# Three short segments of A moved from GpSimd's queue to Sync's, in fp32, in a tiled matmul with leaky ReLU

## The chip, the cores and the metric

One core of one Trainium2 chip. The metric is the device time of one execution in microseconds (us), slowest core, here the only one.

## The reference

```python
m, k, n = 4096, 4096, 4096
a = randn(m, k).astype(float32); b = randn(k, n).astype(float32); alpha = 0.01

def reference(a, b, alpha):
    x = np.matmul(a, b)
    return np.where(x > 0, x, alpha * x)
```

The kernel multiplies in bf16 and accumulates in fp32; 8192 matmuls of 128x128 by 128x512 are needed.

## The kernel before

The output is cut into regions of 512 rows by 1024 columns. The contraction of 4096 is cut into *segments*; the first unit of 1024 is split into two short segments of 512, so that the first two regions can begin early:

```python
SEGS = [(0, 0, 4), (0, 4, 4), (1, 0, 8), (2, 0, 8), (3, 0, 8)]   # unit, first chunk, chunks
TURNS = [(0, [0]), (1, [0]), (0, [1]), (1, [1, 2]), (0, [2, 3]), (1, [3, 4]), (0, [4])]
WHERE = {1: [4, 4, 4, 4], 2: [2, 2, 4, 4], 4: [3, 5, 5, 5]}
```

`TURNS` is the order in which the first two regions (half h of the rows, 0 or 1) take their segments s. One pair (h, s) is a *step*; A(h, s) is its part of A. The first step is (0, 0), the second (1, 0), the third (0, 1), the fourth (1, 1), the fifth (1, 2). A short step is 32 matmuls, a long one 64.

The first step is loaded by Sync and ScalarE's queue in fp32 and rounded by DVE and ScalarE. Everything after it comes over GpSimd's queue, which rounds fp32 to bf16 in the transfer (its packet records before the change hold 1.57 MB of 256-byte writes for the 3.15 MB of fp32 of the three short segments). A is turned ahead of the matmuls: four strips of 32 partitions each are loaded, and DVE transposes 32x32 blocks of pairs of bf16 values (0.42 us for 128x256 pairs).

```python
def load_a(mb, h, s, mt, tiles):
    ...
    def fetch():
        a16 = a16_pool.tile([P, 4 * tiles, kw // 4], BF16, name="a16")
        for q in range(4):
            src = a[row:row + tiles * P, k0 + q * kw // 4:k0 + (q + 1) * kw // 4]
            to = a16[32 * q:32 * q + 32]
            nc.gpsimd.dma_start(to, src.rearrange("(g i) w -> i g w", i=32))
        held.append(a16)

    def turn(t0=0, t1=tiles):
        dst = new_a(mb, h, u)[...]
        nc.vector.transpose(dst..., held[0][:, 4 * t0:4 * t1, :]...)
    return fetch, turn

def load_b(pi, n, s, c):
    u, c0, _ = SEGS[s]
    nc.gpsimd.dma_start(new_b(pi, u)[:, c0 + c, :], b_rows(n, s, c))
```

After a step, `spill` copies its eight PSUM banks out (ScalarE and DVE, or an add on DVE), and the next step may use them. GpSimd starts when A's first rows are rounded, and the second step's strips are turned between the spills of the first:

```python
        if (what, i) == ("a", MT - 1):
            nc.gpsimd.tensor_copy(x[:, :1], a_rounded[:, i, :1])
...
turns[1][0](0, 1)
for mt in range(MT):
    spill(0, mt, banks)
    if mt == 0:
        turns[1][0](1, 2)
turns[1][1]()
for fetch in fetches[2]:
    fetch()
```

In the steps that follow, `WHERE` says behind which group of matmuls the next step's tiles are turned.

## Time and profile before

| | before |
|---|---|
| time, median of the first three runs | 1784.02 us (1783.79 to 1784.41) |
| span in the profile | 1782.6 us |
| TensorE busy | 1775.6 us |
| waits of TensorE from 8.68 us on, all ahead of 47 us | 0.68 + 0.99 + 0.81 = 2.48 us |

A row of a timeline is the start in us, the length, the engine and source line, the operation with its tiles, the count, and in brackets the idle time ahead and what ended it. PE is TensorE, ACT is ScalarE, DVE is VectorE, POOL is GpSimd and SP is Sync; a q behind a name is that engine's queue of instructions. A CAST rounds fp32 to bf16. A transfer *lands* when its last byte is there and whoever waits for it may go on; its packets are the single pieces that the profile records. The granted clock is the share of full speed at which TensorE ran. A profile is one execution; its first 7 us vary by about half a microsecond from one to the next, so the start times of two profiles are compared with that in mind. The lines that carry the argument stand in the prediction below.

### The profile page before, as it was taken

How to read it: one execution, taken by the hardware profiler on the slowest of the kernel's cores; microseconds unless marked ns; L12 is line 12 of the kernel's file. 1: busy time of each engine (PE TensorE's matmuls, PEld its weight loads, DVE VectorE, ACT ScalarE, POOL GpSimd, SP SyncE). 2: the span in 40 equal slices, each digit the busy share in tenths (PEclk: the TensorE clock that was granted, in tenths of full speed). 3: DMA queues.
4: the chain of work that ended last, by engine and by line, in shares of the span. 5: the costliest groups of instructions: out<-in, count | busy, mean ns of one | idle time of the engine just before them, and what ended most of it. 6: DMA issues, size and time to landing. Idle time of an engine off the chain costs nothing.

```text
span 1782.6 us, 18214 instructions
## 1 busy us (share of the span) xinstructions
PE 1775.6 (100%) x8251; PEld 807.3 (45%) x8251; DVE 147.1 (8%) x141; ACT 150.3 (8%) x267; POOL 372.5 (21%) x679
## 2 busy tenths in 40 slices
PE   9999999999999999999999999999999999999999
PEld 4444444444444444444444444444444444444444
DVE  4530000022000000002200000000220000000000
ACT  2010000000000000000000000000000000000011
POOL 6631200433002020043201202014320110301000
PEclk9999999999999999999999999999999999999999
DMA  9995653988039165398704917449860481835511
GB/s 195 200 246 138 116 132 87 187 128 127 39 95 189 48 119 118 95 195 130 123 26 95 188 48 135 102 103 202 129 121 13 111 173 48 163 73 119 117 48 47
DMA packets 164173, 212.50 MB, mean 119 GB/s; under 512 B 43776, under 2 KB 93056, under 8 KB 164096
## 3 DMA queue, kind: packets, MB, share of 16 engines
q0 software_dynamic: 143360, 141.08, 49.9%
q10 hardware_dynamic: 19440, 67.12, 9.7%
q1 hardware_dynamic: 1296, 3.15, 0.5%
q8 instruction: 64, 1.05, 0.2%
q14 instruction: 13, 0.11, 0.0%
HBM read 285.21 MB, written 67.11 MB: 198 GB/s over the span
## 4 chain that ended last, share of the span: by engine, by line
PE 97%; DMA 2%; POOL 1%; issue 0%; SPq 0%; DVE 0%; ACT 0%; POOLq 0%
PE ps L162 97%; DMA bt<-in_b_dram 1%; POOL a L124 1%; DMA a<-in_a_dram 0%; DMA a_in<-in_a_dram 0%; POOL bt L146 0%; SPq L260 0%; DVE a_rounded L267 0%; ACT o L402 0%; POOL x L312 0%; POOLq L312 0%
## 5 line engine op out<-in xcount | busy, mean ns | idle before, releaser
L162 PE MATMUL ps<-bt,at 128*128 128x512 bf16 x8224 | 1769.4, 378 | 2.6 <-DMA bt<-in_b_dram 2.5
L162 PEld LDWEIGHTS <-at 128*128 128x128 bf16 x8224 | 804.3, 98 | 966.8 <-issue 2.5
L146 POOL DMA_DIRECT2D bt<-in_b_dram x412 | 219.3, 539 | 1078.9 <-PE ps L162 1031.9
L385 ACT ACTIVATE o<-ps 128x512 f32<-128x512 f32 x239 | 130.5, 595 | 1511.1 <-PE ps L162 1436.3
L129 DVE STREAM_TRANSPOSE at<-a 128x1024 uint32<-128x1024 uint32 (+2 forms) x83 | 114.5, 1422 | 1152.4 <-DMA a<-in_a_dram 935.7
L124 POOL DMA_DIRECT2D a<-in_a_dram x260 | 152.4, 591 | 200.9 <-DVE at L129 127.2
L240 DVE TENSOR_TENSOR part<-ps,part 128x512 f32<-128x512 f32 x40 | 25.3, 682 | 31.8 <-PE ps L162 31.8
L247 ACT ACTIVATE o<-part 128x1024 f32<-128x1024 f32 x8 | 8.5, 1057 | 100.5 <-DVE part L240 87.3
L92 PE MATMUL wp<-w 128*128 128x512 bf16 x11 | 4.9, 632 | 1.2 <-DVE x L84 1.2
L242 DVE COPY part<-ps 128x512 f32<-128x512 f32 x8 | 5.2, 670 | 1.7 <-PE ps L162 1.7
L244 ACT COPY part<-ps 128x512 f32<-128x512 f32 x8 | 4.4, 593 | 5.9 <-PE ps L162 4.9
L92 PEld LDWEIGHTS <-w 128*128 128x128 bf16 x11 | 1.5, 144 | 3.7 <-issue 2.5
L278 ACT CAST bt<-b_in 128x512 bf16<-128x512 f32 x4 | 2.5, 619 | 3.9 <-DMA b_in<-in_b_dram 3.9
L274 ACT COPY at<-turned 128x512 bf16<-128x512 bf16 x4 | 2.3, 586 | 0.9 <-PE turned L273 0.7
L273 PEld LDWEIGHTS <-a_rounded 128*128 128x128 bf16 x16 | 1.5, 125 | 1.4 <-DVE a_rounded L267 0.9
L273 PE MATMUL turned<-ident,a_rounded 128*128 128x128 bf16 x16 | 2.0, 264 | 0.1
L267 DVE CAST a_rounded<-a_in 128x512 bf16<-128x512 f32 x4 | 1.7, 427 | 4.7 <-DMA a_in<-in_a_dram 4.6
L278 DVE CAST bt<-b_in 128x512 bf16<-128x512 f32 x4 | 1.7, 426 | 2.9 <-DMA b_in<-in_b_dram 2.9
L312 POOL CAST x<-a_rounded 128x1 f32<-128x1 bf16 x1 | 0.2, 183 | 6.7 <-DVE a_rounded L267 6.7
L89 ACT ACT_TABLE_LOAD x1 | 1.3, 1283 | 1.2 <-PEq L421 1.2
L402 ACT ACTIVATE o<-ps 128x256 f32<-128x256 f32 x2 | 0.8, 383 | 6.0 <-PE ps L162 6.0
L82 DVE MEMSET w<- 128x256 uint32 x1 | 0.3, 272 | 0.9 <-PEq L421 0.9
(8 smaller groups left out, 1.2 us busy)
## 6 DMA issues: line engine op xcount, KB each, us to landing
bt<-in_b_dram POOLq DMA_DIRECT2D x412, 256.0 KB, 7.7
out_dram<-o ACTq DMA_DIRECT2D x120, 512.0 KB, 3.9
a<-in_a_dram POOLq DMA_DIRECT2D x244, 128.0 KB, 5.3
out_dram<-o ACTq DMA_DIRECT2D x14, 256.0 KB, 2.0
b_in<-in_b_dram SPq DMA_DIRECT2D x3, 512.0 KB, 6.7
a_in<-in_a_dram SPq DMA_DIRECT2D x4, 256.0 KB, 5.0
a<-in_a_dram POOLq DMA_DIRECT2D x16, 64.0 KB, 3.1
b_in<-in_b_dram ACTq DMA_DIRECT2D x1, 512.0 KB, 4.7
```

The source lines that it names most:

```text
L92: nc.tensor.matmul(wp, w[:, :P], w, start=True, stop=True)
L124: nc.gpsimd.dma_start(to, src.rearrange("(g i) w -> i g w", i=32))
L129: nc.vector.transpose(dst.rearrange("p c m e -> p c (m e)").bitcast(U32) .rearrange("p c (g i) -> p g c i", i=32), held[0][:, 4 * t0:4 * t ...
L146: nc.gpsimd.dma_start(new_b(pi, u)[:, c0 + c, :], b_rows(n, s, c))
L162: nc.tensor.matmul(ps, plain(t)[:, c, rows] if (mb, h, u) == (0, 0, 0) and c < kc0 else t[:, c // 2, rows, c % 2], bt[pi, u][:, c, cols or ...
L240: nc.vector.tensor_add(kept, banks[mt, nt], kept)
L242: nc.vector.tensor_copy(kept, banks[mt, nt])
L244: nc.scalar.copy(kept, banks[mt, nt])
L247: nc.scalar.activation(o, part[h][:, mt, :], LRELU, alpha=alpha)
L273: nc.tensor.transpose(turned[:, c, :], cols[:, c, :], ident)
L278: copy(b0[:, i, columns(nt)], b_in[:, i, columns(nt)])
L385: nc.scalar.activation(o[:, cols], banks[mt, nt], LRELU, alpha=alpha)
```

## The change

The intent is to relieve GpSimd's queue, whose issues hold up B in the first 47 us (7.35 us of them stand ahead of B's second segment). A(1, 0), A(0, 1) and A(1, 1) come over Sync in fp32; ScalarE rounds them; GpSimd's loads begin behind the last strip of A(1, 0), so that they do not disturb it. The core of the diff:

```diff
-WHERE = {1: [4, 4, 4, 4], 2: [2, 2, 4, 4], 4: [3, 5, 5, 5]}
+WHERE = {1: [2, 2, 3, 3], 2: [1, 1, 3, 3], 4: [3, 5, 5, 5]}
...
+    def load_short_a(h, s, staged, tiles):
+        ...
+        def fetch():
+            for mt in range(0, MT, tiles):
+                row = (h * MT + mt) * P
+                for q in range(4):
+                    src = a[row:row + tiles * P, k0 + q * kw // 4:k0 + (q + 1) * kw // 4]
+                    to = staged[32 * q:32 * q + 32, 4 * mt:4 * (mt + tiles), :]
+                    nc.sync.dma_start(to, src.rearrange("(g i) w -> i g w", i=32))
+        def turn(t0, t1):
+            if not held:
+                held.append(a16_pool.tile([P, 4 * MT, kw // 4], BF16, name="a16"))
+            strips = slice(4 * t0, 4 * t1)
+            nc.scalar.copy(held[0][:, strips, :], staged[:, strips, :])
+            transpose(new_a(0, h, u), s, t0, held[0][:, strips, :])
+        return fetch, turn, held
...
+    short = {
+        (1, 0): load_short_a(1, 0, a_both[:, 1], 2),
+        (0, 1): load_short_a(0, 1, a_more[:, 0], MT),
+        (1, 1): load_short_a(1, 1, a_more[:, 1], MT),
+    }
-        made = pieces_a(0, h, s, 2 if i in (1, 3) else None) if i else []
+        made = [] if i == 0 else [short[h, s][:2]] if (h, s) in short else pieces_a(0, h, s)
...
-        if (what, i) == ("a", MT - 1):
-            nc.gpsimd.tensor_copy(x[:, :1], a_rounded[:, i, :1])
...
     turns[1][0](0, 1)
     for mt in range(MT):
+        if mt + 1 < MT:
+            turns[1][0](mt + 1, mt + 2)
         spill(0, mt, banks)
-        if mt == 0:
-            turns[1][0](1, 2)
-    turns[1][1]()
+    nc.gpsimd.tensor_copy(x[:, :1], short[1, 0][2][0][:, 4 * MT - 1, :1])
```

(The staging tiles `a_both` and `a_more` take slots of the pool of B; the transpose is moved into a helper of its own. Both are left out here.)

More of the change, by code (lines that the diff above doesn't have):

```diff
@@ L110, in k_of, with transpose @@
         return (u * KC + c0) * P, kc * P
+    def transpose(at_tile, s, mt, a16):
+        _, c0, kc = SEGS[s]
+        rows = slice(mt * P, mt * P + 32 * a16.shape[1])
+        dst = at_tile[:, c0 // 2:(c0 + kc) // 2, rows, :]
+        nc.vector.transpose(
+            dst.rearrange("p c m e -> p c (m e)").bitcast(U32)
+            .rearrange("p c (g i) -> p g c i", i=32),
+            a16.rearrange("p g w -> p (g w)").bitcast(U32)
+            .rearrange("p (g j c) -> p g c j", j=32, c=kc // 2),
+        )
     def load_a(mb, h, s, mt, tiles):
@@ L127, in turn @@
         def turn(t0=0, t1=tiles):
-            dst = new_a(mb, h, u)[:, c0 // 2:(c0 + kc) // 2, (mt + t0) * P:(mt + t1) * P, :]
-            nc.vector.transpose(
-                dst.rearrange("p c m e -> p c (m e)").bitcast(U32)
-                .rearrange("p c (g i) -> p g c i", i=32),
-                held[0][:, 4 * t0:4 * t1, :].rearrange("p g w -> p (g w)").bitcast(U32)
-                .rearrange("p (g j c) -> p g c j", j=32, c=kc // 2),
-            )
-        return fetch, turn
+            transpose(new_a(mb, h, u), s, mt + t0, held[0][:, 4 * t0:4 * t1, :])
+        return fetch, turn
+    def load_short_a(h, s, staged, tiles):
+        u, c0, kc = SEGS[s]
+        k0, kw = k_of(s)
+        held = []
+        def fetch():
[12 more added lines that the diff above has]
+        return fetch, turn, held
     def b_rows(n, s, c):
@@ L221 @@
     finals = [max(i for i, step in enumerate(steps) if step[0] == h) for h in range(HALVES)]
+    a_rounded = at_pool.tile([P, MT, kw0], BF16, name="a_rounded", tag="at")
+    a_both = bt_pool.tile([P, 2, 4 * MT, P], FP32, name="a_in", tag="bt")
+    a_in = a_both[:, 0].rearrange("p (m q) w -> p m (q w)", m=MT)
+    b0 = new_b(0, 0)
+    a_more = bt_pool.tile([P, 2, 4 * MT, P], FP32, name="a_more", tag="bt")
+    short = {
[3 more added lines that the diff above has]
+    }
     fetches = []
@@ L248, in spill @@
             nc.scalar.dma_start(place(0, h, pairs[0], mt), o)
-    a_rounded = at_pool.tile([P, MT, kw0], BF16, name="a_rounded", tag="at")
-    a_in = bt_pool.tile([P, MT, kw0], FP32, name="a_in", tag="bt")
     order = [("b", 0)] + [("a", mt) for mt in range(MT)] + [("b", c) for c in range(1, kc0)]
@@ L263 @@
     a0 = new_a(0, 0, 0)
-    b0 = new_b(0, 0)
     def round_a(i):
```

## The prediction

> **What bounds the kernel now.** I read the page's busy table first, then the chain that ended last in order of time, then TensorE's timeline of the first 60 us, then GpSimd's.
>
> ```profile
> span 1782.6 us, 18214 instructions
> PE 1775.6 (100%) x8251; PEld 807.3 (45%) x8251; DVE 147.1 (8%) x141; ACT 150.3 (8%) x267; POOL 372.5 (21%) x679
> ...
> 36.93 9.96 DMA bt<-in_b_dram
> 46.89 0.04 issue
> 46.94 1732.53 PE ps L162 x8058
> ```
>
> The last lines are from the chain. From 46.94 us on it is TensorE alone: 8058 matmuls in 1732.53 us, 215 ns each, with no wait to the end. The change touches only the first two regions and is over before then, so the whole question is **when the matmul that started at 46.94 us starts afterwards**. Call that time T; the new time is 1784.02 - (46.94 - T). Nothing behind it can get shorter.
>
> TensorE's timeline shows what can be won before it:
>
> ```profile
> 8.68 13.45 PE L162 MATMUL ps<-bt,at 128*128 128x512 bf16 x60
> 22.81 13.97 PE L162 MATMUL ps<-bt,at 128*128 128x512 bf16 x64 [0.68 <-DMA bt<-in_b_dram]
> 37.77 8.36 PE L162 MATMUL ps<-bt,at 128*128 128x512 bf16 x38 [0.99 <-DMA bt<-in_b_dram]
> 46.94 13.33 PE L162 MATMUL ps<-bt,at 128*128 128x512 bf16 x61 [0.81 <-DMA bt<-in_b_dram]
> ```
>
> The brackets hold the idle time before a group: 0.68 + 0.99 + 0.81 = **2.48 us**, all for loads of B that GpSimd issues. So T is at the least 46.94 - 2.48 = 44.46, and the change is worth 2.5 us at most, 0.14% of the time.
>
> GpSimd's timeline says why B is late:
>
> ```profile
> 8.01 0.18 POOL L312 CAST x<-a_rounded 128x1 f32<-128x1 bf16 x1 [6.70 <-DVE a_rounded L267]
> 8.59 7.35 POOL L124 DMA_DIRECT2D a<-in_a_dram  x12 [0.40 <-issue]
> 15.93 2.18 POOL L146 DMA_DIRECT2D bt<-in_b_dram  x4
> ...
> 31.89 2.29 POOL L146 DMA_DIRECT2D bt<-in_b_dram  x4
> 34.69 1.86 POOL L146 DMA_DIRECT2D bt<-in_b_dram  x3 [0.51 <-DMA a<-in_a_dram]
> 36.93 0.54 POOL L146 DMA_DIRECT2D bt<-in_b_dram  x1 [0.38 <-DMA a<-in_a_dram]
> ```
>
> Twelve short loads of A cost 7.35 us of issue (0.61 us for each 64 or 128 KB) ahead of B's second segment, and more stand ahead of B's third, whose last part is issued at 36.93 and frees TensorE at 46.94. The stretches show what the transfers reach, in written bytes: 402 GB/s in 6.5-10.5 (Sync, fp32), 107 in 11-16 (short A, 256-byte writes, GpSimd 100% busy), 152 in 25.5-28.5 (short A), 194 in 46.5-56 (long A, 512-byte writes), 209 in 36.5-45 (B, 2 KB writes). GpSimd's loads read twice the bytes that they write.
>
> [...]
>
> **The change part by part.**
>
> *Removed from GpSimd*: the three short segments, 16 loads of 64 KB and 4 of 128 KB, 20 x 0.59 = 11.8 us of issue. In transfer time it is 1.57 MB written, at about 140 GB/s some 11 us.
>
> *Added on Sync*: 16 loads, 3 x 1.05 MB fp32 in 512-byte pieces, behind the loads of B's first segment, which end at 10.8 us. The packet records give 84 ns for 2 KB and 159 ns for 4 KB, so about 9 ns + 37.5 ns per KB: 28 ns for 512 bytes, 295 GB/s on 16 engines (an estimate). [...] With 0.7 us from the last byte to the consumer (last packet of b_in 10.84, cast 11.58), the first pair of tiles of A(1,0) is there at 10.7 + 2.2 + 0.7 = 13.6, the second at 15.8, A(0,1) at 20.2, and A(1,1) at 25 to 28, because it shares with B. The built program lets a load wait for the one eight issues earlier; the last of A(1,0) then waits for b_in's landing at 11.5, which still keeps the queue filled.
>
> *Added on ScalarE*: 12 casts 128x512 fp32 to bf16, 0.62 us each by the row of b_in's cast, 7.4 us. ScalarE has room (10.6 us busy of the first 44.5), but the casts stand in its order between the copies that free PSUM banks, 0.59 us each, so a late strip holds up a bank. *DVE*: 12 transposes of 0.42 us, instead of 10 in the same work.
>
> *Moved*: GpSimd begins behind the fourth cast of A(1,0). On ScalarE: two casts 13.6 to 14.84, bank copy to 15.43, cast from 15.8 to 16.42, bank copy to 17.0, cast to 17.63. Then GpSimd's small copy, and 0.4 us as before: first load of B at about 18.3, against 15.93. First bytes 1.5 us later (8.59 to 10.1 before): 19.8, against 18.7.
>
> *Sum for T by the transfers*: [...]the other 0.95 MB take 3.3 us at 295. GpSimd's own, up to the last of B's third segment: B second 1.05 MB / 208 = 5.0, long A 1.05 / 192 = 5.5, B third 2.1 / 208 = 10.1, together 20.6. 19.8 + 3.3 + 20.6 + 0.7 = 44.4. The same sum for before, from 18.7: 20.6 + 3.75 for A(1,1) + 0.7 = 43.8, while it really was 46.9[...]. I take half of it, as the queue mixes fewer small loads: **T about 45.9**, 1.0 us gained.
>
> *Sum by ScalarE and DVE*: A(0,1) at 20.2 has to be cast and turned by 22.1, where its step begins. Two casts (21.4), bank copy (22.0), two casts (23.3), bank copies (23.9, 24.5): tile 3 can start at about 24.5 to 25, where an unbroken TensorE wants it at 23.4. That is 1.1 to 1.6 us of new wait; A(1,1) at 28 would add about 1. They do not add to a later wait for B but take its place, as TensorE then asks later: 44.46 + 1.3 = 45.8, or 46.8 with both. Both sums fall near 46, hence T = 45.9 and 1784.02 - 1.04 = **1783.0 us**.
>
> **The rivals.** (a) *All waits hidden.* If strips run at 295 GB/s, A(0,1) lands at 18.5, no new wait comes up and B's third segment lands before it is wanted: T = 44.5, 1781.5 us. For it: Sync's loads do 402 GB/s and GpSimd was the busiest issuer in that stretch. [...] (b) *The wait is replaced.* [...]if Sync's issue of 256 and 512 pieces takes much more than the 0.45 us of an a_in load, ScalarE is held by strips, banks come free late and GpSimd's start slips past 19: T = 47 to 48.5, 1784 to 1785.5. For it: GpSimd's first B load is later than before even by my own sum. Against: [...]B third needs 10 us of slack only at its last parts. (c) *Nothing moves.* The first 47 us are bound by bytes read, 14 MB, which the change leaves alone: T = 46.9. For it: DMA's busy share is over 1 in every stretch from 5 us. Against: 107 GB/s in 11-16 is an issue limit, not that of the engines.
>
> **Range and chances.** (a) 30%, (c) and my middle case 40%, (b) 30%. The floor is 1781.5 and the bad case about 1785.5; the three runs before lie within 0.6 us. Range 1781.3 to 1785.4. Two per cent is 35.7 us, against 2.48 us to gain and perhaps 4 us to lose in the touched stretch: faster 0.005, same 0.985, slower 0.01.
>
> **What would show it.** In the changed profile: the chain should still end in one run of some 8050 matmuls of 215 ns; its start is T (45.9 by my sum). GpSimd's first B load near 18.3, the first ACT cast of a strip near 13.6, the cast row at 0.62 us. New TensorE waits at 22 to 31 us should name DVE's transpose or a bank, and those for bt at 38 to 47 should shrink below 1.8 in sum. It is wrong if waits come up after 47 us, if Sync's issues take over 1 us each, or if the written rate in 11-19 us is under 150 GB/s.

The rate that was taken for the strips gave the 2.2 us for half a segment in the 13.6 above, the times 15.8 and 20.2, and the 2.2 of 3.15 MB that Sync was to have moved by 19.8 us, which left the 0.95 MB. These times, and GpSimd's start at 18.3 that follows from them, are not worked out from a trace. The 3.1 us between 43.8 and the real 46.9: half of these 3.1 us was taken. The sum itself came to 19.8 + 3.3 + 20.6 + 0.7 = 44.4, so with that half T about 45.9, and 1783.0 us. Rival (a) loses what spoke against it, rival (b) the first of its two conditions, a low rate of the strips, and half of what spoke against it.

## The result, and the profile after

The changed kernel takes **1788.88 us** (median of 6, 1788.62 to 1789.45), against 1784.57 of the kernel before in its six runs (1783.79 to 1786.72). The ratio is 1.0023, with a 95% interval of 1.001 to 1.0036. Such a ratio is the mean time of one kernel's runs over that of the other's of the same rounds, so not quite the ratio of the medians that are quoted. It is within 2% of before, but slower, by about 4.3 us.

First the span, then TensorE's timeline of the changed kernel:

```profile
span 1787.7 us, 18212 instructions
```

```profile
9.12 5.85 PE L192 MATMUL ps<-bt,at 128*128 128x512 bf16 x26 [0.21 <-ACT at L313]
15.92 0.38 PE L192 MATMUL ps<-bt,at 128*128 128x512 bf16 x1 [0.95 <-ACT part L286]
...
18.55 5.12 PE L192 MATMUL ps<-bt,at 128*128 128x512 bf16 x23 [0.17 <-DVE part L284]
26.34 5.42 PE L192 MATMUL ps<-bt,at 128*128 128x512 bf16 x18 [2.67 <-DMA bt<-in_b_dram]
32.15 3.18 PE L192 MATMUL ps<-bt,at 128*128 128x512 bf16 x14 [0.39 <-DMA bt<-in_b_dram]
36.31 0.38 PE L192 MATMUL ps<-bt,at 128*128 128x512 bf16 x1 [0.97 <-DVE part L282]
36.91 83.26 PE L192 MATMUL ps<-bt,at 128*128 128x512 bf16 x384 [0.22 <-DVE part L282]
```

The two late waits for B (0.99 and 0.81 us) are gone, as intended, and four new ones of more than a quarter of a microsecond (0.95, 2.67, 0.39 and 0.97 us) stand ahead of 37 us. Counting matmuls (8160 of 128x512 are recorded in both traces) gives the same matmul in both kernels, and how late it is:

| matmul | before | after | later by |
|---|---|---|---|
| 24, in the first step | 13.33 | 13.08 | -0.24 |
| 32, second step begins | 15.05 | 15.92 | +0.87 |
| 56, near its end | 20.23 | 21.78 | +1.55 |
| 64, third step begins | 22.81 | 26.34 | +3.53 |
| 72 | 24.53 | 29.44 | +4.91 |
| 96, fourth step begins | 29.71 | 36.31 | +6.60 |
| 104 | 31.44 | 38.41 | +6.98 |
| 128, fifth step begins | 37.77 | 43.59 | +5.83 |
| 168, and every one to the end | 47.37 | 52.45 | +5.08 |

So the whole difference of the two spans, 5.1 us, is made ahead of 39 us: 7.0 us were lost by then, and 1.9 us of them are won back where the old waits for B's third segment were. (The spans differ by more than the 4.3 us of the medians, for the profiled run of the changed kernel, 1789.45 us, was the slowest of its six.) The prediction's T, 46.94 before, is 46.94 + 5.08 = **52.0**, not 45.9. The last matmuls of the chain that ended last could mislead here:

```profile
45.10 1739.45 PE ps L192 x8090
```

This run begins near the forecast 45.9, but it holds 32 matmuls more than the 8058 of before, because the late waits are gone.

ScalarE's timeline shows when the strips came (L163 casts them) and GpSimd's when B was asked for:

```profile
14.25 1.14 ACT L163 CAST a<-a_in 128x512 bf16<-128x512 f32 x2 [2.07 <-DMA a_in<-in_a_dram]
15.29 0.58 ACT L286 COPY part<-ps 128x512 f32<-128x512 f32 x1
16.82 0.62 ACT L163 CAST a<-a_in 128x512 bf16<-128x512 f32 x1 [0.95 <-DMA a_in<-in_a_dram]
...
22.40 1.14 ACT L163 CAST a<-a_more 128x512 bf16<-128x512 f32 x2 [2.49 <-DMA a_more<-in_a_dram]
...
34.06 2.18 ACT L163 CAST a<-a_more 128x512 bf16<-128x512 f32 x4 [8.03 <-DMA a_more<-in_a_dram]
```

```profile
18.51 0.18 POOL L359 CAST x<-a 128x1 f32<-128x1 bf16 x1 [17.20 <-ACT a L163]
18.63 2.27 POOL L176 DMA_DIRECT2D bt<-in_b_dram  x4
20.85 2.37 POOL L137 DMA_DIRECT2D a<-in_a_dram  x4
```

A(1, 0) is there at 14.25 and 16.82, A(0, 1) at 22.40, and A(1, 1) only at **34.06**. GpSimd issues B at 18.63, close to the forecast 18.3, yet TensorE gets the first of it at 26.34. Two views of the transfers say why. In the stretch 18.7 to 23.1 us, behind GpSimd's issue, one queue alone moves data:

```profile
DMA packets 1664, 0.83 MB, mean 188 GB/s; under 512 B 48, under 2 KB 1664, under 8 KB 1664
...
q1 hardware_dynamic: 1664, 0.83, 124.8%
```

(q1 is Sync's queue, q0 GpSimd's; the columns are packets, MB written, and share of the 16 engines' time.) In the packet records, GpSimd's first data packet starts at 23.2 us, 4.6 us after the issue; before it took 1.5 us, 8.59 to 10.1. Then, in 24 to 29 us, both move:

```profile
q0 software_dynamic: 451, 0.83, 88.0%
q1 hardware_dynamic: 471, 0.24, 24.5%
```

About as many packets of the one as of the other, but B's carry 2 KB and the strips 512 bytes: the strips get 0.24 MB in 5 us, 48 GB/s.

Last, the granted clock. The stretch table of the changed kernel gives busy us and counts of the engines, then the clock:

```profile
26.30:29.20 2.90, 2.86 (x7) 1.02 (x8) 0.41 (x1) 0.00 (x0) 1.16 (x2) 0.51 1.13 219
```

Behind the wait of 2.67 us TensorE ran at half clock (0.51 in this stretch; the records have 0.5 from 25.74 to 29.15), and eight matmuls that take 1.72 us took 3.10: the +1.38 between matmuls 64 and 72.

### The profile page after: what moved, and what is told of

It reads as the page before. It is cut to its first block, busy times and chain, and to the rows that moved or that the text cites. A ratio compares the mean times of both kernels' runs of the same rounds, so it can differ in the third digit from the quotient of the medians.

```text
span 1787.7 us, 18212 instructions
## 1 busy us (share of the span) xinstructions
PE 1777.1 (99%) x8251; PEld 807.1 (45%) x8251; DVE 147.5 (8%) x142; ACT 156.5 (9%) x279; POOL 360.4 (20%) x659
## 3 DMA queue, kind: packets, MB, share of 16 engines
q8 instruction: 64, 1.05, 0.2%
## 4 chain that ended last, share of the span: by engine, by line
PE 97%; DMA 1%; DVE 0%; SPq 0%; issue 0%; ACT 0%; DVEq 0%; ACTq 0%
PE ps L192 97%; DMA a_more<-in_a_dram 1%; DMA a_in<-in_a_dram 0%; SPq L157 0%; DVE at L118 0%; DMA b_in<-in_b_dram 0%; DVE part L282 0%; ACT a L163 0%; ACT o L439 0%; DVEq L118 0%; DVEq L282 0%; ACTq L163 0%
## 5 line engine op out<-in xcount | busy, mean ns | idle before, releaser
L137 POOL DMA_DIRECT2D a<-in_a_dram x240 | 141.0, 595 | 203.1 <-DVE at L118 137.1
L163 ACT CAST a<-a_more 128x512 bf16<-128x512 f32 x8 | 4.5, 615 | 10.5 <-DMA a_more<-in_a_dram 10.5
L163 ACT CAST a<-a_in 128x512 bf16<-128x512 f32 x4 | 2.4, 616 | 3.0 <-DMA a_in<-in_a_dram 3.0
```

Source lines behind the costliest of these rows:

```text
L163: nc.scalar.copy(held[0][:, strips, :], staged[:, strips, :])
```

## The experiments

**Theory 1**: the strips set the pace, for Sync's queue moves them slowly (188 GB/s in 18.7 to 23.1 us), and once GpSimd's loads flow, the DMA engines take one packet of each queue in turn (451 and 471 in 24 to 29 us), which starves 512-byte pieces beside 2 KB ones (48 GB/s). **Theory 2**: what costs is that GpSimd begins 10 us later, at 18.6 instead of 8.6. **Theory 3**: the order of casts and bank copies on ScalarE and DVE holds up the banks. The halved clock is a further candidate. Each run below is beside runs of the kernel before on the same chip, whose median was 1784.69, 1784.65 and 1784.58 us in the three groups (e1 to e4, e5 to e8, e9 to e11). All results were correct.

### e1: GpSimd begins early

```diff
-    nc.gpsimd.tensor_copy(x[:, :1], short[1, 0][2][0][:, 4 * MT - 1, :1])
...
         there[what].append(i)
+        if (what, i) == ("a", MT - 1):
+            nc.gpsimd.tensor_copy(x[:, :1], a_rounded[:, i, :1])
```

> The whole change, but GpSimd's loads begin behind the rounded rows of A as before, near 8.0 us, not behind the first strips. Theory 1 (the DMA engines take one packet of each queue in turn, so Sync's 512-byte strips get one small packet for each 2 KB packet of B, some 48 GB/s as seen at 24 to 29 us of the changed kernel): the strips of the second step are starved while B moves, they land after 20 us and those of the fourth step after 40 us, and the time is 1795 us or more. Theory 2 (what costs is the late start of GpSimd's loads, and the strips come at their own rate): B's second segment is there by 18 us, the wait of 2.67 us goes with the halved clock behind it, and the time is 1783 to 1785 us.

Measured: **1806.07 us**, ratio 1.012 (1.0105 to 1.0135). The kinds of packets in 22 to 28 us, when GpSimd brings long A with 512-byte writes:

```profile
q0 software_dynamic: 1322, 0.64, 77.1%
q1 hardware_dynamic: 1323, 0.66, 53.2%
```

and the two longest waits of TensorE:

```profile
23.38 8.21 PE L192 MATMUL ps<-bt,at 128*128 128x512 bf16 x24 [4.48 <-ACT part L286]
...
51.48 23.81 PE L192 MATMUL ps<-bt,at 128*128 128x512 bf16 x98 [7.81 <-DVE part L282]
```

1322 packets against 1323: one for one. The strips of the second step landed at 22.2 us and those of the fourth at 49.2. Theory 2 alone is out: starting GpSimd at 8.8 us made it 17 us worse. (Part of these 17 us is the clock: behind the waits it was at 0.5 for 20.5 us in all.) The late start is there for a reason, it shields the strips: the second pair of tiles of A(1, 0) was there at 16.82 us with it.

### e2: matmuls of zeros in the wait

```diff
+            if i == 2:
+                for _ in range(10):
+                    nc.tensor.matmul(banks[0, 0], w[:, :P], w, start=True, stop=True)
```

> The changed kernel with ten matmuls of zeros ahead of the third step, in the place of the 2.67 us in which TensorE waited for B's second segment; their result is overwritten. If the granted clock of 0.5 from 25.74 to 29.15 us comes of that idle time, it stays at 1.0 and the time falls by about 1.4 us, to 1787.5. If the clock fell for another reason, the time stays at 1788.9. If what follows waits for strips anyway, the 1.4 us are lost again at the fourth step, and the time stays too, but with the clock at 1.0.

Measured: **1789.33 us**, ratio 1.0026 (1.0011 to 1.0041), so no gain. The stretch table for the same times:

```profile
26.30:29.20 2.90, 1.85 (x9) 0.78 (x8) 1.34 (x3) 0.67 (x2) 0.58 (x1) 1.00 1.11 211
```

The clock stayed at 1.00, so here the drop does come of the idle time (2.67 us without the ten matmuls, 1.05 with them), but removing it won nothing: the third of the branches foreseen. A(1, 1)'s cast began at 33.49 us in this run (34.06 in the changed kernel), and the fourth step waits for it. The halved clock is a symptom here, not a cause of the final time.

### e3: the third short segment back to GpSimd

```diff
-        (1, 1): load_short_a(1, 1, a_more[:, 1], MT),
...
-    ... else pieces_a(0, h, s)
+    ... else pieces_a(0, h, s, 2 if i in (1, 3) else None)
-WHERE = {1: [2, 2, 3, 3], 2: [1, 1, 3, 3], 4: [3, 5, 5, 5]}
+WHERE = {1: [2, 2, 3, 3], 2: [2, 2, 4, 4], 4: [3, 5, 5, 5]}
```

> The third short segment goes back to GpSimd's queue, behind B's second segment; the first two stay on Sync. Theory 1 (alternation starves it on Sync, it landed at 33.9 us): in GpSimd's own order it takes some 4 us and lands at 30 to 32 us, the waits ahead of the fourth step shrink by 1.5 to 3 us, B's third segment comes later by about 2 us, total 1786 to 1787.5. Theory 2 (the late start of GpSimd): the time stays within 0.7 us of 1788.9.

Measured: **1786.55 us** (1785.70 to 1787.90), ratio 1.0011 (0.9996 to 1.0026), as theory 1 had it: 2.3 us below the changed kernel's median. TensorE's timeline has no wait for B's second segment and no half clock:

```profile
16.65 0.38 PE L192 MATMUL ps<-bt,at 128*128 128x512 bf16 x1 [1.33 <-ACT part L285]
...
26.38 0.38 PE L192 MATMUL ps<-bt,at 128*128 128x512 bf16 x1 [0.58 <-ACT part L285]
26.95 13.06 PE L192 MATMUL ps<-bt,at 128*128 128x512 bf16 x59 [0.19 <-DVE part L283]
40.24 8.36 PE L192 MATMUL ps<-bt,at 128*128 128x512 bf16 x38 [0.23 <-DMA bt<-in_b_dram]
```

By counting matmuls, this profile is 2.3 us behind the kernel before at the 56th, in the second step, 3.2 us at the 72nd, behind waits for banks whose copies stood behind the casts of A(0, 1) (from 23.18 us), and 2.1 us from the 168th on. So what is left comes of the late A(1, 0) and A(0, 1), and having the third segment on Sync costs about half of the change's 4.3 us. The run takes away two things at once, though: the third segment's strips beside B, and the loads that Sync had already issued. Sync had only 0.25 MB to move ahead of GpSimd's first data packet, which came 1.4 us after its issue at 19.40 us instead of 4.6. How the half divides between the two is not shown.

### e4: only the second short segment on Sync

```diff
     short = {
-        (1, 0): ..., 
         (0, 1): load_short_a(0, 1, a_both[:, 1], MT),
-        (1, 1): ...,
     }
...
+WHERE = {1: [3, 3, 4, 4], 2: [2, 2, 4, 4], 4: [3, 5, 5, 5]}   # GpSimd begins as in the kernel before
```

> Only the second short segment comes over Sync in fp32; GpSimd begins at 8.0 us as before, with the first short segment, then B's second, then the third short one. Theory 1: against 256-byte packets of GpSimd the strips get a fair share and land by 19 us, before their step wants them at 22; four of GpSimd's issues (2.4 us) are gone ahead of B, so B's second and third segments land about 2 us earlier than before: 1781.6 to 1783. Rival (fp32 strips cost the DMA engines so much that all else is late): the first short segment lands after 16 us, and the time is 1785 or more.

Measured: **1787.63 us**, ratio 1.0017 (1.0 to 1.0034). My expectation missed by 5 us, and the miss was the most useful one:

```profile
9.13 5.85 PE L192 MATMUL ps<-bt,at 128*128 128x512 bf16 x26 [0.19 <-ACT at L310]
18.79 56.56 PE L192 MATMUL ps<-bt,at 128*128 128x512 bf16 x254 [3.80 <-DVE at L118]
```

A(1, 0) was on GpSimd's queue and issued from 8.55 us on as before, but in the packet records its first data packet starts at 14.8 us, 6.2 us later. Until then Sync's earlier loads went ahead: 1.66 MB of them. There was no fair share to be had at the start: in this run GpSimd's queue moved no data for 6.2 us, while loads that Sync had already issued went ahead. The late first segment and a time over 1785 us are what the rival had named. Two more things are to be read here. GpSimd issued eight loads and then waited 4.05 us for a landing: the program lets it have eight in flight (in the changed kernel, too, it issued eight, and the ninth waited 3.26 us for the first to land). And behind the wait of 3.80 us the clock was at 0.5 for 3.4 us, which is part of the loss.

### e5: B's packets halved

```diff
-        nc.gpsimd.dma_start(new_b(pi, u)[:, c0 + c, :], b_rows(n, s, c))
+        for part_of in range(2) if (pi, s) == (0, 1) else [None]:
+            cols = slice(None) if part_of is None else slice(part_of * RN // 2, (part_of + 1) * RN // 2)
+            nc.gpsimd.dma_start(new_b(pi, u)[:, c0 + c, cols], b_rows(n, s, c)[:, cols])
```

> The changed kernel, with each of the four loads of B's second segment on GpSimd's queue cut into two of 512 columns, so that its packets write 1 KB instead of 2 KB. Alternation packet by packet: the rates in the run with the early gate were 170 + 46 GB/s beside 2 KB packets (193 ns for a pair per engine) and 105 + 108 beside 512-byte ones (78 ns), so a pair with 1 KB should take about 116 ns: the strips get some 70 GB/s and B some 141 while both run. Rival, a share by bytes or by time: the strips stay at 46 to 50 GB/s. The third short segment lands 1 to 2 us sooner, B's second up to 1.5 us later; total within 1 us of 1788.9 either way.

Measured: **1788.82 us**, ratio 1.0024 (1.0007 to 1.004), as long as the changed kernel. In 26 to 29 us:

```profile
q0 software_dynamic: 459, 0.42, 82.2%
q1 hardware_dynamic: 461, 0.23, 36.8%
```

459 packets against 461; 0.23 MB in 3 us is 77 GB/s for the strips, against 48 beside 2 KB packets, and 139 GB/s for B. The forecast from alternation was 70 and 141, the rival's 46 to 50. Together with e1 and the changed kernel this shows nearly equal counts of packets beside 512-byte strips at three sizes: 2 KB (451 to 471), 1 KB (459 to 461) and 512 bytes (1322 to 1323). A(1, 1)'s cast began at 30.51 us instead of 34.06, 3.6 us sooner where 1 to 2 were forecast, but TensorE then waited 1.80 us for B's second segment at 32.99. The strips' gain was B's loss, so the time did not move.

### e6: the strips on two queues

```diff
-                    nc.sync.dma_start(to, src.rearrange("(g i) w -> i g w", i=32))
+                    queue = nc.sync if q < 2 else nc.scalar
+                    queue.dma_start(to, src.rearrange("(g i) w -> i g w", i=32))
...
-    for fetch in fetches[1]:
+    for fetch in fetches[1] + [short[0, 1][0], short[1, 1][0]]:
```

> A measurement of the strips' rate, not a better kernel: all twelve strip loads with q 0 and 1 (partitions 0 to 63) stay on Sync, those with q 2 and 3 (64 to 127) are issued by ScalarE after its casts of B, so both partition halves are written at once. [...] The time will be worse than 1789, for ScalarE waits to issue.

The passage gave two outcomes for the strips' rate with both queues running, 270 GB/s or more, or 195 to 215.

Measured: 1788.20 us, one run of unknown state, no worse than the changed kernel, which I had not expected. For the rate, the 40 slices of 11 to 26 us:

```profile
GB/s 184 183 174 190 175 176 171 187 187 186 220 202 178 175 187 213 231 235 277 273 210 182 173 176 176 178 172 180 190 184 187 221 206 178 172 175 179 172 225 249
```

While one queue alone had data in motion, the rate was mostly 171 to 190 GB/s; the later queue again waited for the earlier one, as in e4: ScalarE issued its first strip at 11.51 us, and both are first in motion at 13.9. The packet records show both in motion in five stretches. In four of them the rate stayed near that of one queue: 185 GB/s in 13.9 to 14.8 us, 191 in 15.9 to 17.0, 184 in 21.7 to 22.6 and 175 in 24.5 to 25.3. Only in 17.0 to 18.5 us was it 254 on average, and over the forecast 270 in two slices. One stretch comes near the first outcome, four do not, so what holds the strips' rate down is not decided.

### e7: bank copies ahead of casts

```diff
-WHERE = {1: [2, 2, 3, 3], 2: [1, 1, 3, 3], 4: [3, 5, 5, 5]}
+WHERE = {1: [4, 4, 5, 5], 2: [2, 2, 5, 5], 4: [3, 5, 5, 5]}
...
-    turns[1][0](0, 1)
-    for mt in range(MT):
-        if mt + 1 < MT:
-            turns[1][0](mt + 1, mt + 2)
-        spill(0, mt, banks)
+    # spill 0 and 1, turn 0 and 1, spill 2 and 3, turn 2 and 3
```

> The changed kernel with ScalarE's and DVE's copies out of PSUM ahead of the casts and transposes of strips, where the change had them behind. Theory 1 (the strips' landing sets the pace): 0.5 to 1.2 us come back, mostly at the second step, where TensorE's wait named ScalarE's copy: 1787.7 to 1788.4. Rival (the order of casts and copies is what costs): the waits of 1.8 us in the second step and about 1.5 us ahead of the fourth both go, 1786 or less.

Measured: **1789.07 us**, ratio 1.0025 (1.001 to 1.004): the time did not come back, not even the little that theory 1 allowed.

```profile
16.00 7.08 PE L192 MATMUL ps<-bt,at 128*128 128x512 bf16 x32 [0.75 <-ACT a L163]
27.30 13.23 PE L192 MATMUL ps<-bt,at 128*128 128x512 bf16 x48 [4.22 <-DMA bt<-in_b_dram]
```

The second step now waits for the cast itself, 0.75 us, where the change showed a bank copy, and runs through: at matmul 56 it is 0.96 us behind the kernel before, where the changed kernel was 1.55. Then TensorE waits for B all the longer, 4.22 us, and the clock is at 0.5 for 6.8 us behind it (3.4 in the changed kernel), so that 48 matmuls take 13.23 us instead of some 10.3 (48 x 215 ns). A(1, 1)'s cast began at 35.13 us. Theory 3 falls as the main cause, for the better order gave the second step some 0.6 us and B's landing took them back; what the order is worth at full clock was not measured. The names of the releasers, bank copies and adds, were those of the last in a row of which the strip's landing was the first.

### e8: the kernel before with fewer, larger loads

```diff
-        made = pieces_a(0, h, s, 2 if i in (1, 3) else None) if i else []
+        made = pieces_a(0, h, s, 2 if i == 1 else None) if i else []
```

> Not the change but the kernel before, with the third short segment loaded in four transfers of 128 KB instead of eight of 64 KB. If the kernel before loses time to GpSimd's issues and the limit of eight transfers in flight, not to bytes, B's third segment lands up to 2 us sooner and the waits of 0.99 and 0.81 us shrink: 1782.5 to 1784. If bytes bound it, the time stays within 0.5 us of before.

Measured: **1783.28 us** (1782.93 to 1783.56), ratio 0.9992 (0.9976 to 1.0009). More on it under e11.

### e9: Sync empty when GpSimd begins

```diff
-        (0, 1): load_short_a(0, 1, a_more[:, 0], MT),
+        (0, 1): load_short_a(0, 1, a_both[:, 1], MT),
```

> A measurement, meant to be slow: the second short segment uses the same buffer as the first, so Sync can issue it only when ScalarE has read the first, about when GpSimd begins. Sync then has nothing in flight when GpSimd issues its first load of B. If the 4.6 us from that issue to its first bytes in the changed kernel are a queue of Sync's earlier strips (0.86 MB moved in between), they shrink to 1.5 to 2.5 us here. If a GpSimd load needs as long when it begins late, they stay at 4.5. The strips of the third step then share with B packet by packet, land after 30 us, and the time is 1795 or more.

Measured: 1803.92 us, one run of unknown state, slow as meant. GpSimd issued B at 18.71 us, and its first data packet started at 20.5: **1.8 us instead of 4.6**. The same stretch as above, 18.7 to 23.1:

```profile
q0 software_dynamic: 147, 0.27, 43.0%
q1 hardware_dynamic: 922, 0.46, 37.7%
```

where the changed kernel had none of q0. So the late first bytes come of what Sync had already issued, not of a late start as such. e3, with a start at 19.40 us and 1.4 us to the first data packet, says the same. The counts agree: when GpSimd's first data packet started, Sync had moved 4962 of the 5120 small packets of the loads that it had issued in full before GpSimd's first issue (changed kernel), 3893 of 4096 in e3.

### e10: only the first short segment on Sync

```diff
     short = {
         (1, 0): load_short_a(1, 0, a_both[:, 1], 2),
-        (0, 1): ...,
-        (1, 1): ...,
     }
...
+WHERE = {1: [4, 4, 4, 4], 2: [2, 2, 4, 4], 4: [3, 5, 5, 5]}
```

> One part of the change alone: only the first short segment on Sync, the other two on GpSimd's queue, which begins behind the first's last strip as in the change. The second step loses the same 1.6 to 2.3 us by its late strips as with two segments on Sync; Sync's queue is empty by 16 us, so GpSimd's bytes start 1.5 to 2 us after its first issue near 19, but it has the second segment to carry ahead of B: B's second lands some 3 us later than in the kernel before. If the late first segment and the late start are what is left of the loss, the time is 1786.5 to 1788.5; if the fp32 form of the second segment is what is left of it, the time is 1785 or less.

Measured: **1790.14 us** (1789.17 to 1790.63), ratio 1.0031 (1.0017 to 1.0045), the slowest of the parts and 1.6 us above the upper end of what I expected. GpSimd's bytes began 1.5 us after its issue, as forecast, but:

```profile
27.52 15.34 PE L192 MATMUL ps<-bt,at 128*128 128x512 bf16 x64 [3.58 <-DVE at L118]
43.77 8.36 PE L192 MATMUL ps<-bt,at 128*128 128x512 bf16 x38 [0.91 <-DMA bt<-in_b_dram]
```

The third step waited 3.58 us for A(0, 1), and its group of 64 matmuls took 15.34 us where before 13.97 were enough: half clock again (0.5 from 26.91 us for 3.4 us), 1.4 us that I had left out. Here the late start does cost, as theory 2 says: Sync's queue was empty from about 16 us on, and GpSimd's had no bytes before 20.4. So theory 2 is right as a part: with the start held at 18.6, the second segment is late if it is left to GpSimd; with the start at 8.8 (e1), the strips are.

### e11: both short segments of the kernel before in larger loads

```diff
-        made = pieces_a(0, h, s, 2 if i in (1, 3) else None) if i else []
+        made = pieces_a(0, h, s) if i else []
...
-    turns[1][1]()
+    turns[1][0](2, 4)
```

> The kernel before with both two-part short segments loaded in four transfers of 128 KB instead of eight of 64 KB. The third segment alone gave 1783.3. With the first too, GpSimd issues B's second segment 2.4 us sooner, but the first tile waits for half a megabyte instead of a quarter: up to 0.5 us lost at the second step, 0.6 us of the wait for B gained: 1782.3 to 1783.5. If the first segment's half comes over 1 us too late, it is back at 1784 or more.

Measured: **1783.14 us** (five runs, 1782.84 to 1783.31), ratio 0.9993 (0.9978 to 1.0007), beside 1784.58 (1783.90 to 1784.99) of the kernel before.

```profile
16.18 0.39 PE L162 MATMUL ps<-bt,at 128*128 128x512 bf16 x1 [1.02 <-DVE at L129]
16.75 43.54 PE L162 MATMUL ps<-bt,at 128*128 128x512 bf16 x201 [0.18 <-DVE part L242]
```

All three waits for B are gone, for one of 1.02 us at the second step. e8 reached the same with 0.63 us for B and 0.38 us for a transpose. Both profiles have a span of 1781.1 us, against 1782.6. The ranges of their runs and of the kernel before do not overlap, though the intervals of the ratios just include 1: about 1.4 us by the medians, not proven by that measure. These are the fastest of all versions run, and they keep everything on GpSimd's queue, with four or eight issues fewer. Whether that relieves GpSimd's issues or its limit of eight loads in flight was not separated.

## Why the prediction was wrong, point by point

**Right.** The change works in the first 50 us alone, and the chain ends in one run of matmuls with no wait (8090 of them in 1739.45 us, 215 ns each). The waits for B's third segment, 1.8 us, went. The cast took 0.62 us, and GpSimd's first issue came at 18.63 (18.3 forecast); that is partly luck, for the fourth cast ended 0.8 us late (18.44 against 17.63) and the first load followed the small copy's start after 0.12 us instead of 0.58. Rival (b), "the wait is replaced", had the direction and half of the reason: the strips were slow (196 GB/s in 11 to 18 us) and came late. But GpSimd's start did not slip past 19, holding up ScalarE was not the main cause (e7), and its size, T at 47 to 48.5, was too small against 52.0.

**The signs.** No wait came up after 47 us, and the strips were written at 196 GB/s in 11 to 18 us, so by these the prediction was not wrong. But the largest new wait in 22 to 31 us, 2.67 us, named B and not a transpose or a bank, and five of Sync's eight loads of the second and third segment took 1.15 to 1.40 us to issue, over the 1 us set as a sign. These issues cost nothing that shows: Sync's packets have no gap above 0.4 us until 33.6 us. One reading of the trace before was wrong, too: it took the 414 GB/s in 5 to 10 us for Sync and Activation together, but they are Sync's alone (739 of 740 packets), for the last packet on Activation's queue ended at 5.04 us.

**Step 1 that failed: the rate of the strips.** The forecast took 2.2 us for half a segment, 0.52 MB. The trace has 196 GB/s in 11 to 18 us and 188 in 18.7 to 23.1: there 1664 packets in 4.4 us, which over 16 engines is one per 42 ns, where the prediction estimated 28. A(1, 0) landed 0.7 and 1.0 us later than forecast (14.25 and 16.82 against 13.6 and 15.8), A(0, 1) 2.2 us (22.40 against 20.2). The rate was my choice, below the estimate of 295 GB/s from the packet times; the measured rates lie below both, and e6 does not decide why. By e3 the late first two segments cost about 2 us in the end.

**Step 2 that failed: "First bytes 1.5 us later".** 1.5 us was measured beside few large packets (some 150 of 4 KB). Behind Sync's backlog it was 4.6 us, with 0.86 MB of Sync's moved in between (4.9 and 1.39 MB in e1, 6.2 and 1.66 MB in e4), and e9 with a nearly empty Sync queue has 1.8; 1.4 us (e3) was the least seen. B's second segment came at 26.3 us; with the forecast 1.5 us it would have been some 3 us sooner (an estimate: 4.6 - 1.5).

**Step 3 that failed: how the queues share.** I let Sync's strips finish at their own rate of 295 GB/s beside B, and A(1, 1) at "25 to 28". They go packet for packet, 451 to 471, so the strips had 48 GB/s, and A(1, 1) came at 34.06. I took it that the queues work side by side, and did not ask in what unit they share. By e3 against the changed kernel, this step and step 2 together are worth about 2.3 us.

**Step 4 that failed: "they do not add to a later wait for B but take its place".** As a principle it held: 1.9 us were won back by the 168th matmul. But at its peak TensorE was 6.98 us behind the kernel before, which itself had waited 0.68 us by then, while I had put the new waits at 1.3 us, or 2.3 with A(1, 1).

**Not foreseen: the halved clock**, 1.4 us at the third step. It came in a wait of 2.67 us and lasted 3.4 us (25.74 to 29.15), while 2.87 us of waiting in e5 were followed by no drop, so the length of the wait alone does not tell. It did not decide the time: e2 and e5 kept the clock at 1.0 there and ended where the changed kernel did. It came again, at 0.5, behind the waits of 3.58 us and more in e1, e4, e6, e7, e9 and e10 and made them dearer.

**What stays open.** The parts do not add: over the kernel before of the same group, the first segment alone on Sync loses 5.6 us by the medians (e10), the second alone 2.9 (e4), the first two 1.9 (e3), all three 4.3. Each part moves the time at which two queues meet, so the shares above are those of single runs, not terms of a sum. Why GpSimd's queue waited behind Sync's backlog at its start (4.6 us), but got as many packets as Sync's later (451 to 471), was not settled; the counts do not tell how many packets make up one turn. Nor was settled what limits the strips' rate (e6).

## What to carry to other kernels

Moving transfers to another queue took 20 loads of some 0.59 us of issue each off GpSimd here, but the two queues then moved packets in nearly equal numbers (451 and 471), so that pieces of 512 bytes got 0.24 MB beside 0.83 MB in mostly 2 KB packets, and what was already queued went first: ask which packets will be in flight together, before asking who issues them. Fewer and larger loads on the same queue were the cheaper cure here, and the only versions below the kernel before, by some 1.4 us. And a wait that names a bank copy may begin with a transfer two steps ahead: e7 removed the named wait and the time stayed.
